# A query block's scores in one matmul over both parts of the keys, and GpSimd's products on VectorE

## The chip, the cores and the metric

The kernel runs on one core of a Trainium2 chip. A core has TensorE (matmuls into PSUM, eight banks of 128 partitions x 512 fp32), VectorE, ScalarE and GpSimd for element-wise work, and SyncE, which issues the loads. Each engine takes its instructions in order and waits for the others by semaphores. The metric is the device time of one execution in microseconds; the figure is the median of three runs.

## The reference

Two layers, each a half-step SwiGLU FFN, a token-mixing sub-layer and a second half-step FFN, on 256 tokens of 1024 channels. Only the mixing sub-layer is touched, and of it the attention and the merge:

```python
def sliding_window_attention(q, k, v, sinks):
    ...
    scores = jnp.einsum('bnqgrd,bnkgd->bngrqk', qb, k2) * scale
    ...
    scores = jnp.where(valid[None, :, None, None], scores, MASK_VALUE)
    m = jnp.maximum(scores.max(axis=-1), sink)
    p = jnp.exp(scores - m[..., None])
    probs = p / (p.sum(axis=-1) + jnp.exp(sink - m))[..., None]
    out = jnp.einsum('bngrqk,bnkgd->bnqgrd', probs, v2)
...
        merged = (jax.nn.sigmoid(g_a) * (y_attn @ w_attn_branch[l])
                  + jax.nn.sigmoid(g_b) * (y_sgu @ w_sgu_branch[l]))
```

There are 16 query heads and 2 key heads of 64 channels, and the window is 128 keys. The 256 queries form two blocks of 128: block n = 0 sees only its own 128 keys, block n = 1 sees 256.

## The kernel before

Every fp32 matrix is used as two parts, a high part (a cast to fp32r) and a low part (what the cast left out), and a product is three matmuls: high by high, high by low, low by high. Weights come as units of 128 x 1024. SyncE loads a unit into one of four `raw` buffers, ScalarE casts the high part (L140), VectorE subtracts for the low part (L154), and that subtraction frees the buffer for the next load. This runs seven units ahead of the unit in use (`AHEAD`, in `st.upto`).

The middle of the mixing sub-layer (`Mix.middle`) is a list of 48 products, eight units each for u, q, gb, the SGU branch, ga and the attention branch. Beside each product stand two half-steps: work put at part 0 is issued ahead of its matmuls, work at part 1 behind them, and `st.upto` for the next unit comes last. Everything else is a generator: `yield k` means "go on k half-steps later". The order on each engine is thus fixed by the written half-steps, and it is the order in which the engine executes.

The attention is six calls of `attend(g, n, heads)`, which start at the half-steps of `ATTEND`, 27, 32, 38, 44, 50, 56. I number them 1 to 6. Calls 1 and 4 are block n = 0 with all eight heads of a key head; calls 2, 3, 5, 6 are block n = 1 with four heads each. A call goes through these steps, with their half-steps counted from its start:

- 0: scores. The keys lie transposed, `kth` the high part, `ktl[0]` and `ktl[1]` the low parts for even and odd heads. For each of the two head parities r there is one PSUM bank; per head one matmul with `kth` (L736) and one with `ktl[r]` (L737) add up in it.
- 3: maxima. One VectorE instruction per head (L743) adds the mask, writes the masked scores to `p` in SBUF and their maximum, not below the head's sink, to `m`; then `nm = -m` (L747) and `sk` (L749).
- 4: ScalarE's exponentials, one per head (L756), each with its sum, and one for `sk` (L758).
- 7: VectorE adds `dn` (L761) and takes the reciprocal `rd` (L763); GpSimd multiplies `p` by it (L764).
- 11: TensorE transposes `p` (L773), ScalarE and VectorE split it in two parts (L171, L172).
- 16: the product with the values, PV (L785, L786), in one or two banks.
- 18 to 21: ScalarE and VectorE turn these into `yah`, `yal` (L796, L799, L802, L804).

The other work in this stretch: the products of q fill banks that ScalarE and VectorE empty into `qs` (L887, L890); the products of gb and of the SGU branch leave two banks (one per block of 128 tokens) after every four units, for half of the 1024 columns, which ScalarE copies out (L905). `gate_b` has ScalarE take the sigmoid of gb and GpSimd multiply `so` by it (L918), in slots 31 and 33; `merge` has VectorE multiply the attention branch by the sigmoid of ga (L937) and GpSimd add `so` (L938), and two products later TensorE transposes the result.

All PSUM banks come from one pool of eight. A new tile takes the bank that was given back first, when the program is written; the first matmul into it then waits until the last reader of the tile before is done.

Of the kernel before, what the change touches and what calls it, by code (L numbers as in the profile page):

```python
# [14 lines left out]
F32R = mybir.dt.float32r  # L15
# [50 lines left out]
def trunk(ctx: ExitStack, tc: tile.TileContext, a: dict, out: bass.AP):  # L66
# [146 lines left out]
    def bank():  # L213
        return new(mm, [P, 512], "mm")
# [446 lines left out]
    class Mix:  # L661
# [29 lines left out]
        def prepare(self):  # L691
            vs = new(n8, [P, NT, D], "n8")
            vv = new(kvp, [P, NT, NKV, 2, HD], "vv", F32R)
            kth = new(kvp, [P, NKV, S], "kth", F32R)
            self.into = (vs, vv, kth, ktl, gain("sgu_ln_g", self.l), gain("sgu_ln_b", self.l))

        def lhs(self, c):
# [22 lines left out]
        def attend(self, g, n, heads):  # L720


            _, vv, kth, ktl = self.into[:4]
            l, qs_, yah, yal = self.l, self.qs, self.yah, self.yal
            nh = len(heads)
            order = heads[0::2] + heads[1::2]
            nk = (n + 1) * P
            qs = rows_of(n)
            half = nh // 2
            s = [bank().rearrange("p (a b) -> p a b", a=half) for _ in range(2)]  # L730
            for i in range(half):
                for r in range(2):


                    q_ = qs_[r][:, heads[0] // 2 + i, qs]
                    nc.tensor.matmul(s[r][:, i, :], q_, kth[:, g, 0:nk], start=True, stop=False)  # L736
                    nc.tensor.matmul(s[r][:, i, :], q_, ktl[r][:, g, 0:nk], start=False, stop=True)  # L737
            yield 3
            m = new(tiny2, [P, 8], "m")
            p = new(t4, [P, nh, nk], "t4")  # L740
            mk = mask.rearrange("p a b -> p (a b)")[:, 256 - nk:]
            for i, hd in enumerate(order):
                nc.vector.tensor_tensor_reduce(out=p[:, i, :], in0=s[i // half][:, i % half, :], in1=mk, scale=1.0,  # L743
                                               scalar=sinks[:, l, hd:hd + 1], op0=ALU.add, op1=ALU.max,
                                               accum_out=m[:, i:i + 1])
            nm = new(tiny2, [P, 8], "nm")
            nc.vector.tensor_scalar(out=nm[:, :nh], in0=m[:, :nh], scalar1=-1.0, scalar2=None, op0=ALU.mult)  # L747
            sk = new(tiny2, [P, 8], "sk")
            nc.vector.tensor_tensor(  # L749
                out=sk[:, :nh].rearrange("p (r j) -> p r j", r=2),  # L750
                in0=sinks[:, l, heads[0]:heads[0] + nh].rearrange("p (j r) -> p r j", r=2),
                in1=nm[:, :nh].rearrange("p (r j) -> p r j", r=2), op=ALU.add)
            yield 1
            sm = new(tiny2, [P, 8], "sm")
            for i in range(nh):
                nc.scalar.activation(p[:, i, :], p[:, i, :], AF.Exp, bias=nm[:, i:i + 1],  # L756
                                     accum_out=sm[:, i:i + 1])
            nc.scalar.activation(sk[:, :nh], sk[:, :nh], AF.Exp)  # L758
# [4 lines left out]
            nc.vector.reciprocal(rd[:, :nh], dn[:, :nh])  # L763
            nc.gpsimd.tensor_tensor(out=p, in0=p, in1=rd[:, :nh].unsqueeze(2).to_broadcast([P, nh, nk]),  # L764
                                    op=ALU.mult)
            yield 4
            parts = []
            for i0 in range(0, nh, 4):

                for c in range(n + 1):  # L770
                    ps = bank()
                    for i, hd in enumerate(range(i0, i0 + 4)):
                        nc.tensor.transpose(ps[:, i * P:(i + 1) * P], p[:, hd, c * P:(c + 1) * P], ident)  # L773
                    ph, pl = new(t2, [P, 512], "t2", F32R), new(t2, [P, 512], "t2", F32R)
                    split(ph, pl, ps)
                    parts.append((i0, c, ph, pl))
            yield 5
            outs = []
            for i0, c, ph, pl in parts:
                if c == 0:  # L780
                    o = bank()
                    outs.append((i0, o.rearrange("p (a b) -> p a b", a=4)))

                v = vv[:, c, g].rearrange("p r d -> p (r d)")
                nc.tensor.matmul(o, v, ph, start=(c == 0), stop=False)  # L785
# [12 lines left out]
            for own, other, o in sides:  # L798
                nc.vector.tensor_tensor(out=y[own], in0=o[own], in1=y0[own], op=ALU.add)  # L799
            yield 1  # L800
            js = slice(heads[0] // 2, heads[0] // 2 + half)
            nc.scalar.copy(yah[:, js, qs], y)  # L802
            yield 1
            nc.vector.tensor_tensor(out=yal[:, js, qs], in0=y, in1=f(yah[:, js, qs]), op=ALU.subtract)  # L804

        def middle(self, xt, xth, xtl, turn1, early):
# [363 lines left out]
```

## Time and profile before

| | us |
|---|---|
| median of 3 runs (1179.13 to 1179.55) | 1179.42 |
| the profiled execution | 1180.49 |
| its span from first to last instruction | 1178.8 |
| TensorE busy in windows 236 to 270, 270 to 348, 348 to 376 (the middle of layer 1's mixing) | 34.0, 78.0, 28.0 |
| VectorE busy in the same | 28.1, 61.9, 21.3 |
| ScalarE busy in the same | 17.9, 60.5, 16.9 |
| GpSimd busy in the same | 0.0, 19.3, 3.5 |

A row of the page or of a group reads: line, engine, operation, tiles written and read, shapes, count, then busy time in us and the mean ns of one, then the idle time ahead of them and who ended it. A row of a timeline reads: start in us from the span's start, duration, engine, line, operation, tiles, and in brackets the idle time ahead and who ended it. A matmul's duration contains its pipeline, so how fast matmuls follow each other is read from their starts, not from their durations. VectorE and ScalarE also begin an instruction shortly before the one ahead of it has ended. Layer 1's attention lies at 270 to 350 us, layer 2's 581 us later, with the same pattern.

### The profile page before, as it was taken

Reading aid. Unit: us, or ns where it says so; the run is one execution under the profiler, and the core shown is the slowest. Engines: PE = TensorE matmul, PEld = TensorE weight load, DVE = VectorE, ACT = ScalarE, POOL = GpSimd, SP = SyncE. Lnnn points to the kernel's source line nnn. Section 1 sums busy time; section 2 is a strip of 40 time slices with the busy share of each in tenths; the row PEclk is TensorE's granted clock in tenths of the full one; section 3 lists DMA queues with packets and bytes.
Section 4 is the critical chain, followed back from the end, with each engine's and each line's share of the span. In section 5 each row is a group of like instructions: output and inputs, shape, how many; then the busy total and the mean of one; then the engine's idle time right before and its main releaser. Section 6 shows DMA issues by size and latency. Waiting matters only on the chain.

```text
span 1178.8 us, 16939 instructions
## 1 busy us (share of the span) xinstructions
PE 1167.2 (99%) x6295; PEld 1007.7 (85%) x6295; DVE 839.7 (71%) x1423; ACT 676.8 (57%) x1139; POOL 59.9 (5%) x44
## 2 busy tenths in 40 slices
PE   8999999999999999999999999999999999999997
PEld 7888888999888888888888888889988888888886
DVE  6768757888787866766586666579778787676752
ACT  5657544557785455655455665455577854566551
POOL 0000000001131100000000000000021220000000
PEclk9999999999999999999999999999999999999999
DMA  7566674555457435657635667645554672565560
GB/s 250 179 242 224 229 234 162 177 181 163 159 161 250 143 140 197 200 196 259 223 106 178 232 199 248 208 152 180 178 167 142 210 222 84 179 212 198 195 199 36
DMA packets 61283, 220.81 MB, mean 187 GB/s; under 512 B 7056, under 2 KB 7056, under 8 KB 61200
## 3 DMA queue, kind: packets, MB, share of 16 engines
q1 hardware_dynamic: 60912, 219.46, 56.1%
q8 instruction: 50, 0.82, 0.3%
q14 instruction: 33, 0.27, 0.1%
q10 hardware_dynamic: 288, 0.27, 0.1%
HBM read 218.65 MB, written 1.05 MB: 186 GB/s over the span
## 4 chain that ended last, share of the span: by engine, by line
PE 98%; DVE 1%; DMA 0%; ACT 0%; issue 0%; SPq 0%; DVEq 0%
PE mm L254 51%; PE mm L284 34%; PE mm L261 3%; PE mm L262 3%; PE mm L263 3%; PE mm L219 2%; PE mm L773 1%; PE mm L737 1%; PE mm L736 1%; PE mm L706 1%; DMA raw<-in_ffn_w 0%; PE mm L786 0%; PE mm L785 0%; DVE t L1079 0%; ACT xt L1003 0%; DVE xt L1006 0%
## 5 line engine op out<-in xcount | busy, mean ns | idle before, releaser
L154 DVE TENSOR_TENSOR wl<-raw,wh 128x1024 fp32r<-128x1024 f32 x372 | 455.0, 1248 | 93.7 <-ACT wh L140 92.2
L140 ACT CAST wh<-raw 128x1024 fp32r<-128x1024 f32 x372 | 383.8, 1051 | 162.0 <-DMA raw<-in_ffn_w 78.0
L254 PE MATMUL mm<-wh,m 128*128 128x512 f32 x1088 | 341.7, 391 | 0.0
L284 PE MATMUL mm<-xt,wh 128*128 128x512 f32 x1152 | 290.5, 393 | 0.7 <-DVE xt L1006 0.7
L254 PEld LDWEIGHTS mm<-wh,m 128*128 128x128 f32 x1088 | 204.3, 188 | 41.9
L284 PEld LDWEIGHTS mm<-xt,wh 128*128 128x128 f32 x1152 | 207.2, 189 | 38.4 <-DVE xt L1006 1.2
L254 PE MATMUL mm<-wl,m 128*128 128x512 f32 x544 | 211.8, 389 | 0.0
L284 PEld LDWEIGHTS mm<-xt,wl 128*128 128x128 f32 x1152 | 157.1, 190 | 11.3
L284 PE MATMUL mm<-xt,wl 128*128 128x256 f32 x1152 | 160.6, 282 | 0.0
L254 PE MATMUL mm<-wh,xt 128*128 128x512 f32 (+1 forms) x480 | 144.1, 378 | 0.0
L651 DVE TENSOR_TENSOR t<-mm,t 128x256 f32<-128x256 f32 x144 | 60.7, 421 | 96.3 <-ACT t L650 96.2
L254 PEld LDWEIGHTS mm<-wl,m 128*128 128x128 f32 x544 | 102.2, 188 | 20.6
L254 PEld LDWEIGHTS mm<-wh,xt 128*128 128x128 f32 x480 | 88.4, 188 | 16.0
L254 PE MATMUL mm<-wl,xt 128*128 128x512 f32 (+1 forms) x240 | 87.5, 375 | 0.0
L650 ACT COPY t<-mm 128x256 f32<-128x256 f32 x144 | 53.0, 368 | 46.4 <-PE mm L284 46.2
L261 PE MATMUL mm<-xt,wh 128*128 128x256 f32 x256 | 73.3, 286 | 0.0
L653 ACT ACTIVATE t<-t 128x256 f32<-128x256 f32 x72 | 30.1, 418 | 74.3 <-DVE t L651 74.3
L263 PE MATMUL mm<-xt,wl 128*128 128x256 f32 x256 | 72.4, 283 | 0.0
L262 PE MATMUL mm<-xt,wh 128*128 128x256 f32 x256 | 72.4, 283 | 0.0
L254 PE MATMUL mm<-m,xt 128*128 128x512 f32 x216 | 54.5, 397 | 0.0
L254 PEld LDWEIGHTS mm<-wl,xt 128*128 128x128 f32 x240 | 45.2, 188 | 7.8
L764 POOL TENSOR_TENSOR t<-t,rd 128x1024 f32<-128x1024 f32 x12 | 26.0, 2170 | 506.4 <-DVE rd L763 488.7
(150 smaller groups left out, 1093.1 us busy)
## 6 DMA issues: line engine op xcount, KB each, us to landing
raw<-in_ffn_w SPq DMA_DIRECT2D x264, 512.0 KB, 4.4
raw<-in_w_in SPq DMA_DIRECT2D x84, 512.0 KB, 3.9
raw<-in_w_sgu_branch SPq DMA_DIRECT2D x16, 512.0 KB, 3.6
raw<-in_w_attn_branch SPq DMA_DIRECT2D x16, 512.0 KB, 3.9
raw<-in_w_out SPq DMA_DIRECT2D x16, 512.0 KB, 4.5
gain<-in_ffn_post_g SPq DMA_DIRECT2D x4, 512.0 KB, 6.7
gain<-in_ffn_pre_g SPq DMA_DIRECT2D x3, 512.0 KB, 5.9
x<-in_x SPq DMA_DIRECT2D x4, 256.0 KB, 4.5
```

What stands on the lines that cost most here:

```text
L140: nc.scalar.copy(h, self.raw[u])
L154: nc.vector.tensor_tensor(out=lo, in0=self.raw.pop(u), in1=f(h), op=ALU.subtract)
L219: nc.tensor.transpose(ps[:, k, :], src[:, (c0 + k) * P:(c0 + k + 1) * P], ident)
L254: nc.tensor.matmul(o, every[i][0], every[i][1], start=start and i == 0, stop=stop and i == 2)
L261: nc.tensor.matmul(o, wh[:, ks], ah[:, k, :], start=(k == 0), stop=False)
L262: nc.tensor.matmul(o, wh[:, ks], al[:, k, :], start=False, stop=False)
L263: nc.tensor.matmul(o, wl[:, ks], ah[:, k, :], start=False, stop=(k == KD - 1))
L284: nc.tensor.matmul(out_, w[:, k * P:(k + 1) * P], x, start=(i == 0), stop=(i == len(todo) - 1))
L650: nc.scalar.copy(y[:, half, :], o[half][:, S:2 * S])
L651: nc.vector.tensor_tensor(out=y[:, half, :], in0=o[half][:, 0:S], in1=y[:, half, :], op=ALU.add)
L653: nc.scalar.activation(y[:, 0, :], y[:, 0, :], AF.Silu)
L764: nc.gpsimd.tensor_tensor(out=p, in0=p, in1=rd[:, :nh].unsqueeze(2).to_broadcast([P, nh, nk]), op=ALU.mult)
```

## The change

The keys get one tile `keys` with three planes: low part for r = 0, high part, low part for r = 1. Two neighbouring planes are then one moving operand. In calls 1 and 4 each head is one matmul of 256 columns (two planes of 128) in place of two of 128 columns. The two sums stay side by side in the bank, so these calls need four banks instead of two. VectorE adds one sum and the mask into `p` (one instruction for two heads, L755 of the changed kernel), and the instruction of the maxima then adds the other sum. The steps of such a call: the scores of r = 0 at 0, of r = 1 at 1, additions and maxima of r = 0 at 2, of r = 1 at 3, and from there as before. Calls 2, 3, 5 and 6 keep their matmuls and maxima. In all calls `p*rd` goes from GpSimd to VectorE, as do `so*gb` (now one instruction for both token blocks) and the sum of the merge.

```diff
-            kth = new(kvp, [P, NKV, S], "kth", F32R)
...
+            if n == 0:
+                s = []
                 for r in range(2):
+                    s.append([bank().rearrange("p (a c b) -> p a c b", a=2, c=2) for _ in range(2)])
+                    for i in range(half):
+                        nc.tensor.matmul(s[r][i // 2][:, i % 2], qs_[r][:, heads[0] // 2 + i, qs],
+                                         keys[:, r:r + 2, g, 0:nk], start=True, stop=True)
+                    yield 1
+                p = new(t4, [P, nh, nk], "t4")
+                for r in range(2):
+                    for i in range(0, half, 2):
+                        at = r * half + i
+                        nc.vector.tensor_tensor(out=p[:, at:at + 2, :], in0=s[r][i // 2][:, :, 0, :],
+                                                in1=mask[:, 1:2, :].to_broadcast([P, 2, P]), op=ALU.add)
+                    if r == 0:
+                        maxima(range(half))
+                        yield 1
+                maxima(range(half, nh))
...
-            nc.gpsimd.tensor_tensor(out=p, in0=p, in1=rd[:, :nh].unsqueeze(2).to_broadcast([P, nh, nk]),
+            nc.vector.tensor_tensor(out=p, in0=p, in1=rd[:, :nh].unsqueeze(2).to_broadcast([P, nh, nk]),
                                     op=ALU.mult)
...
-                for t in range(NT):
-                    nc.gpsimd.tensor_tensor(out=so[:, t, b], in0=so[:, t, b], in1=gb[:, t, b], op=ALU.mult)
+                nc.vector.tensor_tensor(out=so[:, :, b], in0=so[:, :, b], in1=gb[:, :, b], op=ALU.mult)
...
-                nc.gpsimd.tensor_tensor(out=y, in0=y, in1=so[:, t, b], op=ALU.add)
+                nc.vector.tensor_tensor(out=y, in0=y, in1=so[:, t, b], op=ALU.add)
...
-    ktl = [new(const, [P, NKV, S], f"ktl{r}", F32R) for r in range(2)]
+    keys = new(const, [P, 3, NKV, S], "keys", F32R)
+    kth, ktl = keys[:, 1], (keys[:, 0], keys[:, 2])
```

How this moves the instructions is seen at three places. The first is VectorE in call 1 of layer 1. Before, all eight maxima (L743; the row of 128x1 reads its maximum out) stand in one piece behind two low parts (`wl`), and the evacuation of a pair of q (L890) follows `nm` and `sk`:

```order
L154 TENSOR_TENSOR wl_522_2752<-raw_506_2627,wh_521_2751 128x1024
L154 TENSOR_TENSOR wl_527_2804<-raw_512_2670,wh_526_2803 128x1024
L743 ISA t4_534_2843,m_533_2842<-mm_524_2784,mask_11_123,sinks_9_120 128x128
L743 ISA m_533_2842 128x1
...
L747 TENSOR_SCALAR nm_535_2852<-m_533_2842 128x8
L749 TENSOR_TENSOR sk_536_2854<-sinks_9_120,nm_535_2852 128x8
L890 SCALAR_TENSOR_TENSOR m8_494_2555<-mm_519_2720,m8_494_2555 64x512
L890 SCALAR_TENSOR_TENSOR m8_495_2556<-mm_519_2720,m8_495_2556 64x512
```

Now (L738 are the maxima, L917 the evacuation of q, L774 is `nm`):

```order
L154 TENSOR_TENSOR wl_520_2750<-raw_504_2625,wh_519_2749 128x1024
L755 TENSOR_TENSOR t4_531_2829<-mm_523_2783,mask_11_123 128x256
L755 TENSOR_TENSOR t4_531_2829<-mm_524_2784,mask_11_123 128x256
L738 ISA t4_531_2829,m_522_2782<-mm_523_2783,t4_531_2829,sinks_9_120 128x128
...
L154 TENSOR_TENSOR wl_526_2791<-raw_510_2668,wh_525_2790 128x1024
L917 SCALAR_TENSOR_TENSOR m8_492_2553<-mm_517_2718,m8_492_2553 64x512
L917 SCALAR_TENSOR_TENSOR m8_493_2554<-mm_517_2718,m8_493_2554 64x512
L755 TENSOR_TENSOR t4_531_2829<-mm_528_2796,mask_11_123 128x256
L755 TENSOR_TENSOR t4_531_2829<-mm_529_2797,mask_11_123 128x256
...
L774 TENSOR_SCALAR nm_535_2850<-m_522_2782 128x8
```

The block of r = 0 moved ahead of the second low part, and the block of r = 1, with `nm` behind it, moved past the evacuation of q.

The second place is VectorE ahead of call 4's maxima. Before, `dn` and `rd` of call 3, a low part, call 1's `y` (L799), and the maxima:

```order
L761 TENSOR_TENSOR dn_600_3155<-sm_586_3077,sk_582_3068 128x4
L763 RECIPROCAL rd_601_3157<-dn_600_3155 128x4
L154 TENSOR_TENSOR wl_596_3120<-raw_561_2988,wh_595_3119 128x1024
L799 TENSOR_TENSOR t2_603_3161<-mm_587_3095,t2_602_3160 64x512
L799 TENSOR_TENSOR t2_603_3161<-mm_588_3098,t2_602_3160 64x512
L743 ISA t4_608_3185,m_607_3184<-mm_598_3125,mask_11_123,sinks_9_120 128x128
```

Now:

```order
L788 TENSOR_TENSOR dn_601_3140<-sm_586_3073,sk_582_3064 128x4
L790 RECIPROCAL rd_602_3142<-dn_601_3140 128x4
L791 TENSOR_TENSOR t4_580_3057<-t4_580_3057,rd_602_3142 128x1024
L154 TENSOR_TENSOR wl_596_3116<-raw_561_2984,wh_595_3115 128x1024
L826 TENSOR_TENSOR t2_604_3146<-mm_587_3091,t2_603_3145 64x512
L826 TENSOR_TENSOR t2_604_3146<-mm_588_3094,t2_603_3145 64x512
L755 TENSOR_TENSOR t4_610_3163<-mm_599_3122,mask_11_123 128x256
L755 TENSOR_TENSOR t4_610_3163<-mm_600_3123,mask_11_123 128x256
L738 ISA t4_610_3163,m_598_3121<-mm_599_3122,t4_610_3163,sinks_9_120 128x128
```

The product of call 3 (L791) and the additions are new in this queue; nothing changed places.

The third place is TensorE in call 4. Now the scores of r = 0, one unit of gb (twelve matmuls, of which the first are shown) and the scores of r = 1:

```order
L748 MATMUL mm_599_3122<-keys_12_131,m8_492_2553 128x256 x2
L748 MATMUL mm_600_3123<-keys_12_131,m8_492_2553 128x256 x2
L254 MATMUL mm_578_3043<-wh_538_2888,xt_73_351 128x512
L254 MATMUL mm_578_3043<-wl_539_2889,xt_73_351 128x512
...
L748 MATMUL mm_605_3149<-keys_12_131,m8_493_2554 128x256 x2
L748 MATMUL mm_606_3150<-keys_12_131,m8_493_2554 128x256 x2
```

Before, sixteen matmuls of 128 columns (L736, L737) stood ahead of that unit, and none behind it. `mm_578` is the first token block of gb's second half. Its bank goes to the second score bank of call 5, before and now, and ScalarE's queue there has the same rows in both kernels: the eight exponentials of call 4, that of `sk`, the copy of this bank, two casts of call 3's transposed `p`, and the copy of the second token block.

More of the change, by code (lines that the diff above doesn't have):

```diff
@@ L729, in attend @@
             half = nh // 2
-            s = [bank().rearrange("p (a b) -> p a b", a=half) for _ in range(2)]
-            for i in range(half):
-                for r in range(2):
[L735 to L745, printed above, removed]
+            m = new(tiny2, [P, 8], "m")
+            def maxima(heads_):
+                for i in heads_:
+                    hd = order[i]
+                    if n == 0:
+                        part, rest = s[i // half][i % half // 2][:, i % 2, 1, :], p[:, i, :]
+                    else:
+                        part, rest = s[i // half][:, i % half, :], mask.rearrange("p a b -> p (a b)")
+                    nc.vector.tensor_tensor_reduce(out=p[:, i, :], in0=part, in1=rest, scale=1.0,
+                                                   scalar=sinks[:, l, hd:hd + 1], op0=ALU.add, op1=ALU.max,
+                                                   accum_out=m[:, i:i + 1])
@@ new lines, in attend @@
+            if n == 0:
+                s = []
+                for r in range(2):
+                    s.append([bank().rearrange("p (a c b) -> p a c b", a=2, c=2) for _ in range(2)])
[13 more added lines that the diff above has]
+                maxima(range(half, nh))
+            else:
+                s = [bank().rearrange("p (a b) -> p a b", a=half) for _ in range(2)]
+                for i in range(half):
+                    for r in range(2):
+                        q_ = qs_[r][:, heads[0] // 2 + i, qs]
+                        nc.tensor.matmul(s[r][:, i, :], q_, kth[:, g, 0:nk], start=True, stop=False)
+                        nc.tensor.matmul(s[r][:, i, :], q_, ktl[r][:, g, 0:nk], start=False, stop=True)
+                yield 3
+                p = new(t4, [P, nh, nk], "t4")
+                maxima(range(nh))
```

## The prediction

> **What bounds the kernel now.** I read the page first, then TensorE's own waits, then engine by engine the timeline of the attention stage, since the change lives there.
>
> ```profile
> PE 1167.2 (99%) x6295; PEld 1007.7 (85%) x6295; DVE 839.7 (71%) x1423; ACT 676.8 (57%) x1139; POOL 59.9 (5%) x44
> ```
> The view of waits, for TensorE alone, has two rows of note (who waited, for whom, us, times, longest):
>
> ```profile
> PE mm L254 <- ACT m L140: 1.9, 1, 1.9
> PE mm L1028 <- POOL ident masks.py:199: 1.4, 1, 1.4
> ```
> Both lie in the first 10 us. Behind that TensorE runs without a pause, so matmul time removed from it is saved, unless a new wait eats it. The question is how much room the other engines leave. At one place it is nearly none. The score products of call 5 (layer 1), then ScalarE, in the timeline (start, us, engine, line):
>
> ```profile
> 310.52 0.30 PE L736 MATMUL mm<-kth,m 128*128 128x256 f32 x1
> ```
> ```profile
> 306.61 0.40 ACT L756 ACTIVATE t<-t,nm 128x128 f32<-128x128 f32 x1 [0.98 <-DVE nm L747]
> ...
> 309.81 0.56 ACT L905 COPY n<-mm 128x512 f32<-128x512 f32 x1
> ```
> The matmul at 310.52 opens call 5's second score bank. That bank held the first token block of gb's second half, which the L905 copy empties; the copy ends at 310.37, 0.15 us before. In ScalarE's queue the copy stands behind call 4's eight exponentials, and the first of these sat idle 0.98 us for VectorE's `nm`. So already now this matmul hangs on the chain: VectorE's maxima of call 4, `nm`, eight exponentials and the one of `sk` (3.20 us), copy, bank. In the changed kernel the same bank goes the same way (its second score bank follows the first block of gb), and ScalarE's order is unchanged. What delays `nm` of call 4 delays TensorE.
>
> **The change part by part.** First, what TensorE saves:
>
> ```profile
> 269.85 0.28 PE L263 MATMUL mm<-xt,wl 128*128 128x256 f32 x1
> 269.97 0.22 PE L736 MATMUL mm<-kth,m 128*128 128x128 f32 x1
> ...
> 271.71 0.33 PE L261 MATMUL mm<-xt,wh 128*128 128x256 f32 x1
> 271.88 0.28 PE L262 MATMUL mm<-xt,wh 128*128 128x256 f32 x1
> ```
> A matmul of 256 columns with new weights steps by 0.12 us (269.85 to 269.97). The 16 of 128 columns in call 1 take 269.97 to 271.71, and the next step is 0.17 instead of 0.12: 1.79 us. Eight of 256 columns take 0.96, so 0.83 is saved, in each of four calls: 3.3 us. That the 256 columns are two blocks of 128 no row shows; bounds are 0.12 and the old pair's 0.22 (nothing saved); I take 0.12, from the row of equal columns.
>
> Second, VectorE in call 1 (its own timeline):
>
> ```profile
> 269.81 2.35 DVE L154 TENSOR_TENSOR wl<-raw,wh 128x1024 fp32r<-128x1024 f32 x2
> ...
> 274.49 0.17 DVE L747 TENSOR_SCALAR nm<-m 128x8 f32<-128x8 f32 x1
> 274.70 0.17 DVE L749 TENSOR_TENSOR sk<-sinks,nm 128x8 f32<-128x8 f32 x1
> 274.90 1.39 DVE L890 SCALAR_TENSOR_TENSOR m<-mm,m 64x512 fp32r<-64x512 f32 x2
> 276.32 1.23 DVE L154 TENSOR_TENSOR wl<-raw,wh 128x1024 fp32r<-128x1024 f32 x1
> ```
> and the page's row of an addition of the same shape from PSUM:
>
> ```profile
> L651 DVE TENSOR_TENSOR t<-mm,t 128x256 f32<-128x256 f32 x144 | 60.7, 421 | 96.3 <-ACT t L650 96.2
> ```
> L154 steps by 2.35 - 1.23 = 1.12, the L890 pair by 276.32 - 274.90 = 1.42, and the eight maxima by 274.49 - 272.16 = 2.33. An addition of 128x256 costs at most 0.42 (alone) and at least a quarter of L154's 1.12, 0.28; I take 0.34 in a row of them. The new order is L154, two additions, four maxima, L154, the L890 pair, two additions, four maxima, `nm`: 269.81 + 1.12 + 0.68 + 1.16 + 1.12 + 1.42 + 0.68 + 1.17 = 277.16. So `nm` of call 1, and its exponentials, come 2.67 us later: the L890 pair now stands ahead, and four additions are new.
>
> Third, the product `p*rd` moves to VectorE:
>
> ```profile
> 280.30 0.20 DVE L763 RECIPROCAL rd<-dn 128x8 f32<-128x8 f32 x1
> 280.53 1.39 DVE L890 SCALAR_TENSOR_TENSOR m<-mm,m 64x512 fp32r<-64x512 f32 x2
> ```
> It has L154's shape: 1.12, or 1.25 with nothing beside it. I take 1.12, plus the wait for `rd` where the next instruction did not wait. `dn`, `rd` follow ScalarE's exponentials and casts, hence the 2.67; then 1.12 more, so call 2's maxima and exponentials come 3.8 us later. ScalarE:
>
> ```profile
> 285.98 1.04 ACT L140 CAST wh<-raw 128x1024 fp32r<-128x1024 f32 x1
> 288.25 1.08 ACT L171 CAST t<-mm 128x512 fp32r<-128x512 f32 x2 [1.23 <-PE mm L773]
> ...
> 293.46 0.51 ACT L756 ACTIVATE t<-t,nm 128x256 f32<-128x256 f32 x1 [0.47 <-DVE nm L747]
> ...
> 295.45 0.19 ACT L758 ACTIVATE sk<-sk 128x4 f32<-128x4 f32 x1
> 298.25 1.08 ACT L171 CAST t<-mm 128x512 fp32r<-128x512 f32 x2 [2.61 <-PE mm L773]
> ```
> L140 begins at 289.8, L171 at 290.8 instead of 288.25: the idle stretch takes up part, 2.55 remains. VectorE's half of that split, `dn`, `rd` and call 2's product (1.23, with its wait for `rd`) make call 3's exponentials 3.8 late: ScalarE is free at 295.55 + 3.8 = 299.35. The 2.61 us of idle no longer suffice: L171 begins 1.1 later than 298.25.
>
> Fourth, call 4 on VectorE, which from here on has no pause until `nm`:
>
> ```profile
> 298.87 1.29 DVE L172 TENSOR_TENSOR t<-mm,t 128x512 fp32r<-128x512 f32 x2 [4.16 <-ACT t L171]
> ...
> 301.40 0.18 DVE L763 RECIPROCAL rd<-dn 128x4 f32<-128x4 f32 x1
> 301.49 1.21 DVE L154 TENSOR_TENSOR wl<-raw,wh 128x1024 fp32r<-128x1024 f32 x1
> 302.62 1.40 DVE L799 TENSOR_TENSOR t<-mm,t 64x512 f32<-64x512 f32 x2
> ```
> L172 starts 1.1 late. L154 waited 0.09 behind the start of `rd`; now `rd` ends (0.18 + 0.03), the product takes 1.12, L154 follows: 1.23 more. Then four additions ahead of `nm`: 1.36. Exponentials and copy come 1.1 + 1.23 + 1.36 = 3.7 us late: the copy ends at 314.1, the matmul starts at 314.2 instead of 310.52. Behind the waiting exponentials queue the copy, call 3's two L171 and the second copy; behind the waiting matmul, five more score matmuls and the next product. After this TensorE is late by the same 3.7 as the engines that it waits for, so no wait of that size follows. **Each layer loses 3.7 us net, both layers 7.4.**
>
> The bounds: additions of 0.28 to 0.42 move call 1's `nm` by 0.24 down or 0.32 up, and call 4's by the same; products of 1.12 to 1.25 add up to 0.13 thrice. So 3.2 to 4.7 a layer, 6.4 to 9.4.
>
> Where TensorE pauses: it comes earlier by two savings, 1.67. On the way PV of call 3 waits for L799 (bank of call 1's PV):
>
> ```profile
> 305.77 0.39 PE L785 MATMUL mm<-t,vv 128*128 128x512 f32 x1
> ```
> L799's first half ends at 302.62 + 0.70 + 1.1 + 1.23 = 305.65, TensorE is there at 304.1: 1.5 us. At the bank it arrives at 310.52 - 1.67 + 1.5 = 310.35 and waits until 314.2: **3.8 us of idle TensorE**. That reaches the clock. The windows (us, then busy of PE, PEld, DVE, ACT, POOL, then the granted clock) around the 1.9 us wait of the start, which ended at 8.49:
>
> ```profile
> 8.00:10.00 2.00, 1.51 (x4) 1.06 (x5) 1.53 (x2) 1.00 (x3) 0.00 (x0) 0.74 1.03 421
> 10.00:12.00 2.00, 2.00 (x10) 2.00 (x9) 1.20 (x3) 1.19 (x2) 0.00 (x0) 0.50 0.85 301
> 12.00:14.00 2.00, 2.00 (x9) 1.60 (x9) 2.00 (x3) 1.39 (x2) 0.00 (x0) 0.91 0.41 127
> ```
> Means of 0.74, 0.50 and 0.91 are half clock from 8.96 to 12.36, 3.4 us, after only 1.9 idle. So I expect the same behind 3.8: at most 1.7 us lost (half of 3.4), less where part of the slow stretch falls into the wait. I take 1.4 a layer, 2.8.
>
> [...]
>
> Costed at nothing: `so*gb` and the merge's sum (16 GpSimd instructions become 12 on VectorE). `so` is complete some ten products before its merge, and the merge's sum is followed by its transposes only two products later; if that cover failed, a merge would lose about 0.7, a half of L799's 1.40, which has as many columns. The L154s behind the new work come up to 3.7 late, and with them the release of `raw` buffers to SP's loads; weights are split seven units ahead of their use, which covers it. The scores of r = 1 in call 4 pass behind one product; no load is issued there.
>
> **The sum.** The profiled execution took 1180.49 (span 1178.8, 1.7 around it): 1180.49 + 7.4 + 2.8 = 1190.7. The median of the runs is 1.07 lower: 1179.42 + 10.2 = **1189.6**.
>
> **The rivals.**
> [...]
>
> *Call 1's delay is swallowed before call 4* (0.10): if ScalarE's idle 2.61 suffices, L171 follows TensorE, 0.83 earlier, and only 1.23 + 1.36 - 0.83 = 1.8 a layer is lost, 1183.0. Against it: the 3.8 above. For it: the sum runs through several idle stretches, and each could be wider than I read it.
>
> *Not slower: VectorE gets its time back* (0.08). While GpSimd multiplies, VectorE can be held up:
>
> ```profile
> 313.80 1.90 POOL L764 TENSOR_TENSOR t<-t,rd 128x1024 f32<-128x1024 f32 x1 [9.34 <-DVE rd L763]
> ```
> ```profile
> 314.46 2.32 DVE L154 TENSOR_TENSOR wl<-raw,wh 128x1024 fp32r<-128x1024 f32 x1
> ```
> Here L154 takes 2.32, not 1.23, so a moved product would cost almost nothing. It decides where call 4's copy comes less than 0.83 late against its transposes (TensorE's own gain at call 1). If it were not late at all, each layer would gain 0.83 + 0.15 and the time be 1177.4; the full 3.3 (1176.1) needs the copy 1.5 earlier still. Against it: between 298.87 and 304 no L154 was held up (1.21), though that layer's third product ran on GpSimd then. [...]
>
> **How the numbers follow.** Forecast with the clock falling in both layers: 0.50. Clock holding: 0.29. Swallowed: 0.10. Not slower: 0.08, of it 0.04 faster. Worse, additions and products at their upper ends or a second slow stretch, up to 1194: 0.03. The range takes the swallowed case's edge and the upper bound (9.4 + 3.4 = 12.8): 1183.0 to 1192.0. Within 0.2% (2.4 us, about what a measurement can tell from no change) lie 0.04; slower by more 0.92.
>
> **What would show it.** Right: a pause of over 3 us on TensorE in each layer at call 5's second bank, put down to ScalarE's copy; one of about 1.5 at PV of call 3; the clock below 1 behind it; `nm` of call 1 about 2.7 late; scores at 0.12 a step. Wrong: no wait of TensorE above 1 us there, or the pause without a fall of the clock.

## The result, and the profile after

The changed kernel takes 1190.12 us (median of 4 runs, 1188.91 to 1190.55), the kernel before beside it 1179.49 (4 runs, 1179.13 to 1180.34): a ratio of 1.0088, 95% interval 1.0076 to 1.010. It is slower by 10.6 us; 1189.6 was forecast, with a range of 1183.0 to 1192.0. The profiled execution took 1188.91, its span is 1187.2.

First the page of the changed kernel: busy time of the engines, and the group of the low parts on VectorE.

```profile
PE 1166.9 (98%) x6263; PEld 1005.0 (85%) x6263; DVE 853.3 (72%) x1463; ACT 676.6 (57%) x1139; POOL 7.1 (1%) x16
L154 DVE TENSOR_TENSOR wl<-raw,wh 128x1024 fp32r<-128x1024 f32 x372 | 444.9, 1221 | 95.9 <-ACT wh L140 94.8
```

TensorE has 32 matmuls fewer, VectorE 13.6 us more work, GpSimd next to none. The shares tell nothing of the loss. L154 now takes 1.221 us on the mean and none over 1.23; before it took 1.248, and 14 took 2.0 to 2.4. With GpSimd's products gone no L154 is held up in this run, and still the kernel is slower. TensorE's view of waits (who waited, for whom, us, times, longest) tells where:

```profile
PE mm L768 <- ACT n L932: 6.6, 2, 3.3
PE mm L812 <- DVE t L826: 2.3, 2, 1.2
```

Both rows are new, and each occurs once a layer. In TensorE's timeline these are call 1's scores (layer 1), PV of call 3, and call 5's second score bank in layer 1 and in layer 2:

```profile
269.46 1.12 PE L748 MATMUL mm<-keys,m 128*128 128x256 f32 x8
270.42 0.28 PE L261 MATMUL mm<-xt,wh 128*128 128x256 f32 x1
...
305.61 0.50 PE L812 MATMUL mm<-t,vv 128*128 128x512 f32 x1 [1.16 <-DVE t L826]
...
313.94 0.39 PE L768 MATMUL mm<-keys,m 128*128 128x256 f32 x1 [3.30 <-ACT n L932]
```
```profile
855.22 1.12 PE L748 MATMUL mm<-keys,m 128*128 128x256 f32 x8
...
899.71 0.39 PE L768 MATMUL mm<-keys,m 128*128 128x256 f32 x1 [3.27 <-ACT n L932]
```

The eight scores of call 1 take 269.46 to 270.42, 0.12 a step. From call 1's first score to call 5's second bank the changed kernel needs 313.94 - 269.46 = 44.48 us in layer 1 and 899.71 - 855.22 = 44.49 in layer 2. Before it was 310.52 - 269.97 = 40.55. This distance leaves out where in time a run began, and I use it for all kernels below: **3.93 us a layer are lost here**, 7.9 in all.

The ScalarE work that leads to the bank (layer 1): call 3's L171, call 4's first exponential, and the copy that frees the bank.

```profile
299.26 1.04 ACT L171 CAST t<-mm 128x512 fp32r<-128x512 f32 x2
...
310.14 0.40 ACT L783 ACTIVATE t<-t,nm 128x128 f32<-128x128 f32 x1 [2.25 <-DVE nm L774]
...
313.33 0.56 ACT L932 COPY n<-mm 128x512 f32<-128x512 f32 x1
```

And VectorE, call 1 up to its `nm`, then the stretch ahead of call 4's `nm`:

```profile
269.31 1.22 DVE L154 TENSOR_TENSOR wl<-raw,wh 128x1024 fp32r<-128x1024 f32 x1
270.56 0.76 DVE L755 TENSOR_TENSOR t<-mm,mask 128x256 f32<-128x256 f32 x2
...
272.31 1.22 DVE L154 TENSOR_TENSOR wl<-raw,wh 128x1024 fp32r<-128x1024 f32 x1
273.56 1.39 DVE L917 SCALAR_TENSOR_TENSOR m<-mm,m 64x512 fp32r<-64x512 f32 x2
...
276.86 0.17 DVE L774 TENSOR_SCALAR nm<-m 128x8 f32<-128x8 f32 x1
...
299.86 1.29 DVE L172 TENSOR_TENSOR t<-mm,t 128x512 fp32r<-128x512 f32 x2 [1.44 <-ACT t L171]
...
302.39 0.18 DVE L790 RECIPROCAL rd<-dn 128x4 f32<-128x4 f32 x1
302.60 1.23 DVE L791 TENSOR_TENSOR t<-t,rd 128x1024 f32<-128x1024 f32 x1
303.74 1.22 DVE L154 TENSOR_TENSOR wl<-raw,wh 128x1024 fp32r<-128x1024 f32 x1
```

L171 of call 3 has no idle time ahead of it now: the 2.61 us are used up. VectorE has no gap from L172 on. From the start of `rd` to L154 it now takes 303.74 - 302.39 = 1.35 us, where it took 0.09: call 3's product (L791), with its wait for `rd`, puts L154 and what follows 1.26 us back. The idle time of ScalarE ahead of call 4's exponentials grew from 0.98 to 2.25, waiting for `nm`.

Last the clock, windows around the pause in layer 1 and in layer 2 (us, then busy of PE, PEld, DVE, ACT, POOL, then the granted clock):

```profile
312.00:314.00 2.00, 0.06 (x1) 0.06 (x1) 0.04 (x1) 2.00 (x11) 0.00 (x0) 1.00 0.63 195
314.00:316.00 2.00, 2.00 (x9) 1.81 (x10) 1.59 (x3) 2.00 (x4) 0.00 (x0) 0.65 0.17 68
316.00:318.00 2.00, 2.00 (x6) 1.52 (x6) 1.93 (x4) 1.94 (x4) 0.00 (x0) 0.50 0.19 16
318.00:320.00 2.00, 2.00 (x10) 1.63 (x9) 1.95 (x4) 0.91 (x3) 0.00 (x0) 0.99 0.64 246
```
```profile
898.00:900.00 2.00, 0.29 (x2) 0.30 (x3) 0.00 (x0) 2.00 (x9) 0.00 (x0) 1.00 0.82 233
900.00:902.00 2.00, 2.00 (x13) 1.75 (x13) 1.83 (x3) 2.00 (x4) 0.00 (x0) 1.00 0.07 29
```

In layer 1 means of 0.65, 0.50 and 0.99 are half clock from 314.6 to 318.0. In layer 2, behind a pause of the same length, the clock holds. This is the run of 1188.91 with a mean clock of 0.998; the three others, not profiled, took 1190.08 to 1190.55 at 0.995.

### The profile page after: what moved, and what is told of

The parts are those of the page before. It is cut to its first block, busy times and chain, and to the rows that moved or that the text cites. A ratio compares the mean times of both kernels' runs of the same rounds, so it can differ in the third digit from the quotient of the medians.

```text
span 1187.2 us, 16848 instructions
## 1 busy us (share of the span) xinstructions
PE 1166.9 (98%) x6263; PEld 1005.0 (85%) x6263; DVE 853.3 (72%) x1463; ACT 676.6 (57%) x1139; POOL 7.1 (1%) x16
## 4 chain that ended last, share of the span: by engine, by line
PE 95%; DVE 2%; ACT 1%; DMA 1%; issue 0%; SPq 0%; DVEq 0%
PE mm L254 49%; PE mm L284 34%; PE mm L261 3%; PE mm L262 3%; PE mm L263 3%; PE mm L219 1%; ACT t L783 1%; PE mm L800 1%; DMA raw<-in_ffn_w 1%; PE mm L705 1%; DVE wl L154 0%; PE mm L813 0%; PE mm L812 0%; DVE t L738 0%; PE mm L768 0%
## 5 line engine op out<-in xcount | busy, mean ns | idle before, releaser
L154 DVE TENSOR_TENSOR wl<-raw,wh 128x1024 fp32r<-128x1024 f32 x372 | 444.9, 1221 | 95.9 <-ACT wh L140 94.8
L284 PEld LDWEIGHTS mm<-xt,wh 128*128 128x128 f32 x1152 | 207.3, 189 | 38.6 <-DVE xt L1033 1.2
L262 PEld LDWEIGHTS mm<-xt,wh 128*128 128x128 f32 x256 | 49.1, 192 | 0.0
```

The lines of the kernel that those rows point to most:

```text
L154: nc.vector.tensor_tensor(out=lo, in0=self.raw.pop(u), in1=f(h), op=ALU.subtract)
L262: nc.tensor.matmul(o, wh[:, ks], al[:, k, :], start=False, stop=False)
L284: nc.tensor.matmul(out_, w[:, k * P:(k + 1) * P], x, start=(i == 0), stop=(i == len(todo) - 1))
```

## The experiments

The theory is the prediction's: VectorE's new work delays call 4's maxima, ScalarE's exponentials wait for them, the copy behind these frees call 5's second bank late, TensorE pauses, and the clock falls behind the pause. The kernels were run in three groups, each beside fresh runs of the kernel before (medians 1179.9, 1179.65 and 1179.44). "Distance" is that from call 1's first score to call 5's second bank.

| kernel | median us | ratio to before, 95% | distance, layers 1 and 2 |
|---|---|---|---|
| before | 1179.4 to 1179.9 | 1 | 40.55, 40.55 |
| changed | 1190.12 | 1.0076 to 1.0100 | 44.48, 44.49 |
| scores alone | 1182.18 | 1.0014 to 1.0032 | 40.95, 40.95 |
| p*rd alone | 1182.16 | 1.0009 to 1.0026 | 41.67, 41.67 |
| gates and merge alone | 1179.48 | 0.9989 to 1.0008 | 40.55, 40.55 |
| p*rd alone, not in call 3 | 1179.58 | 0.9984 to 1.0002 | 40.55, 40.55 |
| changed, n = 0 blocks earlier | 1185.94 | 1.0042 to 1.0069 | 42.16, 42.16 |
| changed, call 3's p*rd on GpSimd | 1188.02 | 1.0056 to 1.0082 | 43.17, 43.22 |
| changed, copy first | 1186.45 | 1.0040 to 1.0065 | 41.00, 41.02 |
| changed, repeated scores | 1187.47 | 1.0053 to 1.0078 | 44.49, 44.48 |
| changed, earlier blocks, call 5 later | 1179.25 | 0.9988 to 1.0006 | |
| scores alone, copy first | 1177.53 | 0.9975 to 0.9993 | 38.88, 38.88 |
| scores alone, call 5 later | 1179.15 | 0.9984 to 1.0002 | |
| changed, once more | 1190.47 | 1.0071 to 1.0101 | 44.44, 44.45 |

### The three parts by themselves

Scores alone is the changed kernel with GpSimd's instructions put back:

```diff
-            nc.vector.tensor_tensor(out=p, in0=p, in1=rd[:, :nh].unsqueeze(2)...
+            nc.gpsimd.tensor_tensor(out=p, in0=p, in1=rd[:, :nh].unsqueeze(2)...
...
-                nc.vector.tensor_tensor(out=so[:, :, b], in0=so[:, :, b], in1=gb[:, :, b], op=ALU.mult)
+                for t in range(NT):
+                    nc.gpsimd.tensor_tensor(out=so[:, t, b], in0=so[:, t, b], in1=gb[:, t, b], op=ALU.mult)
...
-                nc.vector.tensor_tensor(out=y, in0=y, in1=so[:, t, b], op=ALU.add)
+                nc.gpsimd.tensor_tensor(out=y, in0=y, in1=so[:, t, b], op=ALU.add)
```

> Only the scores are changed (one matmul over both key parts, additions and the moved block on VectorE); the products stay on GpSimd. Theory (all delay reaches TensorE through call 4's exponentials, ScalarE's copy and call 5's second bank): without the products ScalarE's idle 2.61 us ahead of call 3's L171 swallows call 1's delay, L171 follows TensorE 0.83 earlier, and call 4's four additions make the copy 1.36 - 0.83 = 0.5 late. Loss 0.5 us a layer, TensorE pausing 0.15 less than 0.53 + 1.67, about 2.0 us; 1180.4 us if the clock holds behind 2.0 us, 1183.2 if it falls in both layers (1.4 each). Rival (what VectorE gains or loses is spread, and TensorE's saving stands by itself): 3.3 us faster, 1176.1, and no pause over 1 us.

Measured 1182.18. The pauses, in TensorE's timeline of this kernel:

```profile
270.56 1.12 PE L748 MATMUL mm<-keys,m 128*128 128x256 f32 x8
...
311.51 0.38 PE L768 MATMUL mm<-keys,m 128*128 128x256 f32 x1 [1.92 <-ACT n L932]
```
```profile
893.90 0.39 PE L768 MATMUL mm<-keys,m 128*128 128x256 f32 x1 [1.92 <-ACT n L932]
```

The distance is 40.95, 0.40 longer (0.5 expected), the pause 1.92 (2.0 expected). So the two layers lose 0.8, yet the median lost 2.3. The rest of 1.5 fits the clock: in the profiled run it fell behind one of the two equal pauses only, and the matmuls behind that pause come 1.57 us later than the same ones in layer 2. The windows behind the two:

```profile
312.00:314.00 2.00, 2.00 (x9) 1.67 (x8) 2.00 (x3) 1.98 (x4) 0.00 (x0) 0.57 0.00 0
314.00:316.00 2.00, 2.00 (x7) 1.56 (x6) 1.92 (x6) 1.96 (x5) 1.12 (x1) 0.57 0.24 43
```
```profile
894.00:896.00 2.00, 2.00 (x12) 1.78 (x13) 1.64 (x3) 2.00 (x4) 0.00 (x0) 1.00 0.06 23
```

The time lies between the two cases expected, 1180.4 and 1183.2. The rival, 1176.1 without a pause, falls.

The product alone is one line of the kernel before; in a second kernel call 3 is left out of it:

```diff
-            nc.gpsimd.tensor_tensor(out=p, in0=p, in1=rd[:, :nh].unsqueeze(2)...
+            eng = nc.gpsimd if heads[0] == 4 and n == 1 else nc.vector
+            eng.tensor_tensor(out=p, in0=p, in1=rd[:, :nh].unsqueeze(2)...
```

> Only p*rd goes to VectorE in all calls. Theory: calls 1 and 2 are hidden by ScalarE's idle 2.61 us, call 3's product stands ahead of call 4's maxima: copy 1.23 late less 0.15 of slack, a pause of 1.1 us a layer, clock holds: 1181.6 us. Rival (VectorE gets the time back where GpSimd held up its L154): no more than 0.2 us, 1179.4, and no pause.

> p*rd on VectorE in five of the six calls of a layer; call 3's stays on GpSimd. Theory: only call 3's product stands between ScalarE's exponentials and call 4's maxima, so nothing is lost: 1179.4 us, no pause at call 5's second bank. Rival (every product costs its share): five sixths of what all six cost.

Six products a layer on VectorE cost 2.3 us (1182.16), five cost nothing (1179.58). The row of the first of these kernels:

```profile
310.81 0.39 PE L736 MATMUL mm<-kth,m 128*128 128x256 f32 x1 [0.96 <-ACT n L905]
```

The distance grew by 1.12 a layer (1.1 expected), 2.24 in all, and in the profiled run the clock held. So the whole price of the product is the third one, which stands ahead of call 4's maxima; the other five fit into idle time. The rival, that VectorE gets the time back from L154s that GpSimd held up, falls: the held-up L154 that the prediction shows stands at 314.46, behind call 4's maxima.

> Only so*gb and the merge's sum go to VectorE. Theory: covered, no pause of TensorE, 1179.4 us within 0.5. Rival (part of the loss of 10.6 us comes from here): slower by 0.7 us or more for each of the eight merge steps that is uncovered, over 1181.

Measured 1179.48, no wait: the cover that the prediction named for these instructions holds.

**The parts don't add up.** Alone they cost 2.3, 2.3 and nothing, together 10.6; by the distance, which leaves out the clock behind the pause, 0.40, 1.12 and nothing a layer against 3.93. What comes ahead of call 3's L171 is swallowed by the 2.61 us of idle there when it comes alone: L171 begins 28.28 us behind call 1's first score before, 27.45 with the scores alone and 28.28 with p*rd alone. In the changed kernel it is 29.80: together they overrun the idle time.

### What delays call 4

Two kernels take one link out of the chain of the changed kernel. In the first the additions and maxima of calls 1 and 4 come a half-step earlier:

```diff
-                    yield 1
+                    if r == 0:
+                        yield 1
                 p = new(t4, [P, nh, nk], "t4")
...
-            yield 1
+            yield 2 if n == 0 else 1
             sm = new(tiny2, [P, 8], "sm")
```

> The changed kernel with the n = 0 calls' additions and maxima a half-step earlier, so that call 1's second block stands ahead of the L917 pair as before the change; its exponentials stay at their step. Theory (call 1's delay reaches call 4 through calls 2 and 3): nm of call 1 1.42 us earlier, the wait at PV of call 3 goes, and call 4's chain and the copy come 1.4 to 2.1 earlier in each layer: 1186 to 1187.3, the pause at the bank staying over 3 us. Rival (ScalarE's idle 2.61 swallows call 1's delay, and only call 3's product and call 4's additions count): 1190, within 0.5.

Measured 1185.94, a little better than expected. In three views, call 1's start and call 5's bank on TensorE, `nm` of call 1 on VectorE, L171 of call 3 on ScalarE:

```profile
268.57 1.12 PE L748 MATMUL mm<-keys,m 128*128 128x256 f32 x8
...
310.73 0.39 PE L769 MATMUL mm<-keys,m 128*128 128x256 f32 x1 [3.12 <-ACT n L933]
```
```profile
273.28 0.17 DVE L775 TENSOR_SCALAR nm<-m 128x8 f32<-128x8 f32 x1
...
273.57 1.22 DVE L154 TENSOR_TENSOR wl<-raw,wh 128x1024 fp32r<-128x1024 f32 x1
274.82 1.39 DVE L918 SCALAR_TENSOR_TENSOR m<-mm,m 64x512 fp32r<-64x512 f32 x2
```
```profile
296.03 1.08 ACT L171 CAST t<-mm 128x512 fp32r<-128x512 f32 x2 [0.25 <-PE mm L801]
```

`nm` comes 273.28 - 268.57 = 4.71 us behind call 1's first score; in the changed kernel it is 276.86 - 269.46 = 7.40, so it moved by 2.7 and not by 1.42: I had overlooked that the half-step passes an L154 as well as the evacuation of q (L918 here). L171 waits for TensorE again, so nothing of call 1's delay reaches call 4, and the wait at PV is gone. The distance is 310.73 - 268.57 = 42.16, 1.61 more than before: the price that the prediction gave the case "swallowed" was 1.8. From VectorE's half of that split (L172) to call 4's `nm` it is 10.07 us in both kernels, so the gain comes from call 1. Call 1's delay is thus worth 3.93 - 1.61 = 2.3 us a layer. The rival falls. The wait at the bank stays at 3.1 us, since TensorE also arrives earlier, and the clock still falls behind one pause of the profiled run, which took 1183.71 at a mean clock of 0.998. The other four runs had 0.993 to 0.996.

The second link is call 3's product, left out by the same `eng` line as above:

> The changed kernel with call 3's p*rd on GpSimd, the other five on VectorE. Theory: call 4's chain and L799's counterpart lose 1.23 us each, so the wait at PV of call 3 falls from 1.2 to about 0, and the copy comes 1.23 earlier; TensorE meets it that much earlier too, so the pause at the bank stays 3.4 us. 2.5 us in all: 1190.1 - 2.5 = 1187.6. Rival (ScalarE, which has no idle left ahead of call 3's L171, sets call 4's chain, not VectorE): 1190.

Measured 1188.02. The wait at PV is gone from the view of waits; TensorE's timeline has

```profile
268.31 1.12 PE L748 MATMUL mm<-keys,m 128*128 128x256 f32 x8
...
311.48 0.39 PE L768 MATMUL mm<-keys,m 128*128 128x256 f32 x1 [3.29 <-ACT n L933]
```

so the distance is 43.17, 1.3 us shorter, and the pause stays. Theory right, rival wrong: VectorE, not ScalarE, sets call 4's chain.

### The bank, and what is late next

If the copy L932 makes TensorE wait, putting it ahead of call 4's exponentials takes the wait away. The only edit is the place in a half-step's list:

```diff
-                            at(divmod(half, 2), lambda h=j // 4, t=t, o=o[t], half=half: go(evac(h, t, o), half))
+                            fn = lambda h=j // 4, t=t, o=o[t], half=half: go(evac(h, t, o), half)
+                            at_ = todo.setdefault(divmod(half, 2), [])
+                            at_.insert(0 if first else len(at_), fn)
...
-            quads(self.gb, xth, xtl, lambda h, t, o: rows_to(gb, h, t, o))
+            quads(self.gb, xth, xtl, lambda h, t, o: rows_to(gb, h, t, o), first=True)
```

> The changed kernel with one order turned round: ScalarE's copy of the first token block of gb's second half (and of its first half) ahead of what falls due with it, so ahead of call 4's exponentials. Theory (this copy frees call 5's second score bank): the wait of 3.4 us at that bank goes in both layers; since ScalarE and VectorE stay as late as they were, TensorE meets them again within the next two calls, after at most the idle that ScalarE still has there (1.09, 1.84 and 1.55 us in the trace), so 1.5 to 3.4 us a layer are gained, and the clock's 1.4 where the pause falls under 2 us: 1190.1 becomes 1180 to 1187. Rival (TensorE waits for these engines as a whole, whatever bank stands first): the same 3.4 us turn up at the next instruction, 1190.

Measured 1186.45, inside the range. TensorE's longest wait in this kernel's view:

```profile
PE mm L254 <- DVE t L172: 3.9, 2, 2.0
```

The wait at the bank is gone, so it was this copy. But a wait of 2.0 us a layer, of the 3.3, takes its place a call later, for a bank that VectorE's half (L172) of call 5's split holds:

```profile
325.37 0.72 PE L254 MATMUL mm<-wh,m 128*128 128x512 f32 x1 [1.94 <-DVE t L172]
```

VectorE and ScalarE are still late, and TensorE meets them at the next bank.

With the scores alone there is less lateness to meet:

> Scores alone, as in the first experiment, with gb's copies ahead of what falls due with them on ScalarE. Theory: the 0.5 us by which the copy is late, the pause of 1.92 us and its falls of the clock go, and TensorE's 3.3 us are left: 1179.7 - 3.3 = 1176.4, and no pause over 0.5 us in the attention. Rival (the four additions of a call cost TensorE's saving elsewhere): 1179 to 1182 as before.

Measured 1177.53 against 1179.65, ratio 0.9984 (0.9975 to 0.9993). This is **the one kernel that beats the kernel before**, by about 2 us; the interval leaves out 1, but the gain is within the 0.2% that the prediction took for no change. Its call 5 opens the second bank 38.88 us after call 1's first score, 1.67 less than before: TensorE's whole saving. Its waits:

```profile
PE mm L254 <- DVE t L172: 1.4, 2, 0.7
```

This new wait, 0.7 us a layer where at most 0.5 was expected, is 1.4 in both and covers the 1.1 us that it misses to the forecast 1176.4.

Two kernels go another way: call 5 starts a half-step later, so one more product stands ahead of the bank (`ATTEND` 51 for 50).

> All three changes, the n = 0 blocks a half-step earlier as in the run before, and call 5 a half-step later (51 for 50), so that its scores stand behind one more product, 16 matmuls of 512 columns at 0.227 or 3.6 us. Theory (the pause is a matter of what stands ahead of the bank): the wait of 3.1 us a layer is covered, and no fall of the clock follows; the chain of call 5 starts later, so waits of up to 1 us may come back at its transposes. 1185.9 - 6.2 - 1.4 = 1178, at most 1180. Rival (the moved work costs VectorE's time in the end): a new wait of 2 us or more a layer, as behind the copy put first, over 1181.

Measured 1179.25, inside the theory's 1178 to 1180: all three changes, with the blocks earlier and call 5 later, are level with the kernel before. Two waits at score banks, 0.4 and 0.5 us, are left in each layer, and TensorE's saving doesn't show in the time.

> Scores alone, with call 5 a half-step later instead of the copy put first. Theory: the pause of 1.92 us a layer is covered by the product ahead; without the 0.7 us wait for L172 that the copy put first had, 1179.7 - 3.3 = 1176.4. Rival: call 5's chain, 3.6 us later, meets its transposes or PV: a wait of 0.7 or more, 1177.5 or above.

Measured 1179.15, a miss; the rival's "1177.5 or above" is nearer. In layer 1 no wait is left, in layer 2 there are three:

```profile
PE mm L768 <- ACT n L932: 0.6, 1, 0.6
PE mm L768 <- DVE m L738: 0.3, 1, 0.3
PE mm L812 <- DVE t L826: 0.3, 1, 0.3
```

What differs between the layers is VectorE's L154 and GpSimd's third product beside it, first in layer 1, then in layer 2:

```profile
301.61 1.21 DVE L154 TENSOR_TENSOR wl<-raw,wh 128x1024 fp32r<-128x1024 f32 x1
```
```profile
301.86 2.71 POOL L791 TENSOR_TENSOR t<-t,rd 128x1024 f32<-128x1024 f32 x1 [5.97 <-DVE rd L790]
```
```profile
881.32 2.89 DVE L154 TENSOR_TENSOR wl<-raw,wh 128x1024 fp32r<-128x1024 f32 x1 [0.26 <-issue]
```
```profile
881.24 1.90 POOL L791 TENSOR_TENSOR t<-t,rd 128x1024 f32<-128x1024 f32 x1 [5.95 <-DVE rd L790]
```

Where VectorE starts 0.25 us ahead, GpSimd takes 2.71 instead of 1.90 and nobody waits for it; where GpSimd starts 0.08 ahead, VectorE's L154 takes 2.89 instead of 1.21, just ahead of call 4's maxima. That is 1.7 us (2.0 with L154's later start) in the chain ahead of the three waits, which layer 1 doesn't have. The profiled run also had a longer wait at the start (2.8 us, 1.9 in the kernel before), and as the other runs have no profile, how much of the 2.7 us missed by the median comes from here stays open.

### The clock

Twelve repeats of call 5's first pair of score matmuls, ahead of the bank, fill the pause with work that changes no result:

```diff
+                q_ = qs_[0][:, heads[0] // 2, qs]
+                for _ in range(12 if g == 1 and heads[0] == 8 else 0):
+                    nc.tensor.matmul(s[0][:, 0, :], q_, kth[:, g, 0:nk], start=True, stop=False)
+                    nc.tensor.matmul(s[0][:, 0, :], q_, ktl[0][:, g, 0:nk], start=False, stop=True)
                 for i in range(half):
```

> The changed kernel, with call 5's first score product (a pair of matmuls) written twelve times more, into the same place and ahead of the bank that is waited for: 24 x 0.12 = 2.9 us of work added to TensorE in each layer, in the pause of 3.4, of which 0.6 is left. Theory (the pause ends with ScalarE's copy, whatever TensorE does; the clock falls because TensorE stands idle): the end of the pause stays, no fall of the clock, and the time drops by 1.4 us for each fall that the changed kernel had, one or two: 1187.3 to 1188.7. Rival for the pause (TensorE's own work counts): 5.8 us slower, 1195.9. Rival for the clock (it doesn't follow the idle time): 1190.1.

Measured 1187.47. TensorE does 5.8 us more and the kernel is 2.65 us faster than the changed one. The second bank, and the windows, in layer 1:

```profile
270.35 1.12 PE L748 MATMUL mm<-keys,m 128*128 128x256 f32 x8
...
314.84 0.39 PE L772 MATMUL mm<-keys,m 128*128 128x256 f32 x1 [0.44 <-ACT n L936]
```

```profile
313.00:315.00 2.00, 1.56 (x13) 1.36 (x12) 0.00 (x0) 2.00 (x10) 0.00 (x0) 1.00 0.75 213
315.00:317.00 2.00, 2.00 (x12) 1.78 (x13) 1.70 (x3) 2.00 (x4) 0.00 (x0) 1.00 0.12 49
```

The distance is 314.84 - 270.35 = 44.49, as in the changed kernel: the pause ends with the copy, whatever TensorE does. The clock stays at 1.00 behind it, and so it does in layer 2. The five runs have a mean clock of 0.997 to 0.999. From the second bank to call 1 of layer 2 there are 540.00 us here and 541.28 in the changed kernel, whose profiled run has a fall there: 1.3 us for one fall. So the clock's share of the 10.6 us is about 2.7 (the two ratios' intervals leave some 2 us either way), and in these two runs it went with TensorE's idle time at the bank: no fall behind the two waits of 0.44 us, one behind the two of 3.3.

> The changed kernel itself again, for the clock. Theory: the same two waits in each layer (1.2 and 3.4 us), and half clock for 3.41 us where one window of the clock's own grid of 3.41 us holds more than 1.9 us of TensorE's idle time; which layer that is changes from run to run with the place of the pause on the grid, so 1187 to 1190.5 with the count of falls, and most runs with two.

Measured 1190.47 (1187.72 to 1192.7); the two longest of the five runs, 1190.65 and 1192.7, lie above the range expected, and without a profile of them why stays open. The mean clock was 0.994 to 0.997. The profiled run, 1189.69, has half clock behind both pauses. Layer 2:

```profile
899.00:901.00 2.00, 2.00 (x10) 1.75 (x11) 1.66 (x3) 2.00 (x4) 0.00 (x0) 0.77 0.17 68
901.00:903.00 2.00, 2.00 (x6) 1.55 (x5) 1.93 (x4) 1.94 (x4) 0.00 (x0) 0.50 0.07 18
```

## Why the prediction was right

*What bounds the kernel, and the place of the loss.* The prediction picked one matmul, the one that opens call 5's second bank, and the 0.15 us by which it was not late. There lies the loss, and the copy put first shows that this copy causes it.

*TensorE's saving.* 0.83 us a call was right: 0.96 for eight matmuls of 256 columns, and the full 1.67 a layer in the run with scores alone and the copy first.

*VectorE's chain.* Call 1's `nm` was put 2.67 us late. It came at 276.86 instead of 274.49, in a run whose call 1 began 0.51 earlier: 2.88. Call 3's product with its wait: 1.26 (1.23 taken), additions 0.67 a pair (270.56 to 271.23, where the maxima begin; 0.68 taken). The copy was put 3.7 late; 313.33 - 309.81 + 0.51 = 4.03 was found. Of the 0.3 us too little, call 1's maxima account for 0.2 (the two L154 there step by 1.25, 269.31 to 270.56 and 272.31 to 273.56, where 1.12 was taken), and most of the rest is call 1's product, for which 1.12 was taken too and which steps by 1.25. The matmul came 44.48 - 40.55 = 3.93 late: less than the copy, because the 0.15 us of slack comes off. The prediction let the matmul be as late as its copy and took nothing off. The two errors go opposite ways, so that 3.7 lies within 0.2 of 3.93 is partly luck.

*The pauses.* 1.5 at PV and 3.8 at the bank were expected; 1.16 and 3.30 idle were found, or 1.3 and 3.5 against TensorE's pace, since the view counts a matmul's pipeline as busy (the score matmul at 310.37 stands there with 0.28, where they step by 0.12). A third was overlooked: at call 4's second group of scores TensorE stands in short stops for banks that VectorE's late L172 frees, about 0.7 us in all (300.14 to 301.54, 1.40 us for five steps that take 0.71 at 0.23 and 0.12). The three add up to 5.5 us, about what TensorE saved and what the layer lost, 1.67 + 3.93; without the third the pause at the bank would have been the longer, and the loss the same.

*The clock.* 1.4 us a layer in both layers was the forecast, 2.8; the repeats give 2.65. The step behind it, half clock for 3.4 us behind each such pause, came true behind some pauses and not behind others: the profiled run had one fall and came out at 1188.91, the second profiled run two, at 1189.69. The clock falling in both layers and the clock holding in one are thus the same kernel on different runs; that most runs, by their mean clock of 0.995, had two was not to be told from the one fall at the start. The distance and the repeats' 2.65 add up: 1179.4 + 7.9 + 2.7 = 1190.0, and the median is 1190.1.

*Costed at nothing.* Right for the gates and the merge (1179.48): the view of waits of that kernel has no row for them. The scores of r = 1 in call 4 were put at nothing as well; they are the 0.7 us above.

*The rivals.* "Swallowed" describes the kernel with the n = 0 blocks earlier, at 1.6 a layer for the 1.8 given. But its price of 1183.0 left the clock out, though TensorE's pause is still 3.1 us there; that kernel took 1185.94. "Not slower" falls: the L154s did get their time back (mean 1.248 to 1.221 us), but behind the chain, not in it: in layer 1 all seven that took 2.0 us or more stand at 314.46 or later. The range's upper end, by its own sum, is 1192.2, not 1192.0.

## What to carry to other kernels

Look for the instruction that is barely not waiting (here 0.15 us of slack at one PSUM bank) and follow what it hangs on through every queue: the copy that frees a bank was cheap, but stood behind eight exponentials that waited for another engine. Costs of parts of a change don't add up: each alone mostly fitted into 2.61 us of idle time, and together they did not, so price them together along one chain. Removing a wait on a queue that stays late moves a good part of it, here 2.0 of 3.3 us, by a call; taking work off the chain and starting the consumer later, together, brought the changed kernel back to level.

## What was not expected of the hardware

*When the clock falls.* A stretch of half clock behind a pause lasted 3.41 us: 8.95 to 12.36 in the kernel before, 314.62 to 318.03 in the changed one. In three traces the falls began whole multiples of this apart: in the repeated run of the changed kernel at 313.00 and 900.09, 172 times 3.413; in its first profiled run at 314.62 and, behind the last matmul, at 1185.02, 255 times; in the kernel before at 8.95 and, behind the last matmul, at 1176.30, 342 times. Some falls began during the pause (313.00, where the pause ended at 313.25), some behind it (314.62, where it ended at 313.94). In the cases read here, the falls had TensorE idle for more than half of the 3.41 us ahead: 1.92 us at the start of the kernel before, 2.74 in layer 1 of the changed kernel, and 1.92 in layer 1 of scores alone, where the pause, 309.59 to 311.51, lies inside the stretch that ends at 312.29. In layer 2 of these last two the clock held. Carrying the steps of 3.413 on from layer 1, which is my estimate, a boundary at 898.30 cuts the changed kernel's pause in 1.87 and 1.41, and one at 892.56 cuts that of scores alone in 0.58 and 1.34. So few cases show no exact border. By the starts of the same matmuls in layers 1 and 2, the fall made TensorE 1.57 us late in scores alone and 1.62 in the changed kernel (from call 5's second bank to the next PV, 7.88 us and 6.26).

*VectorE and GpSimd beside each other.* In the kernel with the scores alone and call 5 later, an L154 and a product, both of 128x1024, overlap in both layers. In layer 1 L154 started 0.25 us ahead and took 1.21, the product 2.71; in layer 2 the product started 0.08 ahead and took 1.90, L154 2.89. In each, the one that started first was the one that took no longer than elsewhere. With these 0.3 us between their starts the price was nothing in one layer and 1.7 us on the chain in the other.
